# Seven block products for the attention output projection, with all of adaLN's remaining groups moved beside the retention's projections

## The chip, the cores and the metric

The program runs on one core of one Trainium2 chip. The core has five engines: TensorE (PE in the profile, with its weight loads as PEld), VectorE (DVE), ScalarE (ACT), GpSimd (POOL) and SyncE (SP), and 16 DMA engines. The metric is the device time of one launch in microseconds, the median of several runs.

## The reference

One layer of a hybrid backbone, run for 128 context tokens and 512 latent tokens, 640 in all. Everything is float32. What matters here, cut from the reference:

```
m  = silu(cond) @ w_mod + b_mod            # adaLN: sh1, sc1, g1, sh2, sc2, g2 (1024 columns each)
h  = rmsnorm(x, norm1_g) * (1 + sc1) + sh1
q, k, v, rq, rk, rv, rg, ga, gr = split(h @ w_in)
ya = attend_blocks(q, k_all, v_all)        # 640 x 1024
yr = silu(rg) * rms_scale(retention)       # 640 x 1024
y  = sigmoid(ga) * (ya @ w_att_o) + sigmoid(gr) * (yr @ w_ret_o)
x  = x + g1 * (y @ w_out)
x  = x + g2 * conv_ffn(rmsnorm(x, norm2_g) * (1 + sc2) + sh2)
return rmsnorm(x, final_g)
```

The change touches `ya @ w_att_o` (640 x 1024 by 1024 x 1024), the place of the products `silu(cond) @ w_mod` that are not needed at the start, the end of `yr @ w_ret_o`, and the end of the last normalisation.

## The kernel before

Every float32 product is made of three matmuls on a split: a number is written as a high part that TensorE takes as it is (`fp32r`) and a low part, the rest. `mm3` adds high by high, high by low and low by high into one PSUM bank. `w_split` (L139) makes the two parts of a weight: ACT casts the high part (L145), DVE subtracts it for the low part (L150), or, in the form called "dma", ACT writes the negative high part (L147) and a DMA on POOL's queue adds the weight to it.

**Attention projection** (L795 and around). The attention output is split into `yaT` (high `ya.u1`, low `ya.u2`, transposed, 8 chunks of 128 rows by 640 tokens; ACT L646, DVE L647). The loop over the 8 output columns of 128 takes the weights of two columns at a time and calls `b_col`, which for each half of 320 tokens makes 8 chunks x 3 matmuls of 128x320 into one bank (L195 to L197). `ya_ev` (DVE, L793) multiplies the result by the gate and, behind the second half, writes the column to DRAM (POOL, L795). In each column, `next(ada)` steps the generator `mod_rest` (L235 and on): it loads 2 MB of `w_mod` into its one buffer `wm` (SP, L249), yields six times, makes 32 matmuls (64 on record, L257), and turns the result around with a small matmul (L265). Beside the attention projection it makes four such groups, for `sc2` and `sh2`; four more, for `g1` and `g2`, run beside the projections of rk, rq and rv. `decay_consts` (L580 to L601) is a chain of small operations of 128x16 on DVE that makes the constants of the retention. All of this stands in the order that the scheduler finds: it lets PE go from one bank to another where one waits.

**Retention projection** (`ret_unit`, and its pump, inside `tc.manual_schedule`, so that PE, DVE and ACT run in the order in which the code is written). Pairs of columns, p = 0 to 3, are made by seven block products instead of eight, as in Strassen's method (Winograd's form): the 1024 rows of the weights and the two columns make 2 x 2 blocks, the tokens make two halves, and products 1 to 7 of 12 matmuls each work on sums of blocks. The order in a pair is 1, 5, 6, 2, 3, 7, 4, with 4 held back by two places into the next pair. Products 1, 6, 7 and 4 add up in one bank, 2 in another, 5 and 3 in a third; ACT copies the shared bank out behind each product (L1114, L1118, L1122, L1126), and the next one may add only then. `prep` makes the weights of one product (a sum on DVE, L1063; the cast on ACT, L1073; the low part by DVE, L1082, or by DMA, L1080, for product 3 and for product 2 of p > 0). `ret_pump` runs `load` and `prep` ahead by the room in the `wh` buffers. `col` applies the gates, `merge` splits the result for the next product (ACT L1099, DVE L1100). Behind it comes the output projection with `w_out`; the split of the second half of its first weights (`w_split(wo1[0])`, on ACT L145) is left to the scheduler.

**The end.** `last(t, c0, n)` makes the last matmuls of a token block and a range of columns and calls `down_add` (DVE L1427, L1428) and `square` (ACT L1445); `root_sum` and `root` make the 1/rms of token blocks (DVE L1453 to L1466, the power on POOL), and `out` scales and writes 128x512 (ACT L1479 or DVE L1477; SP L1481).

## Time and profile before

| | us |
|---|---|
| median of 3 runs | 1182.92 (1180.72 to 1183.16) |
| the profiled execution | 1182.97 |
| its span, first to last instruction | 1181.1 |
| PE busy | 1148.8 (97%) |
| DVE busy | 772.9 (65%) |
| ACT busy | 589.6 (50%) |
| POOL busy | 184.6 (16%) |

The rows come from one profiled execution. A row of the timeline is one instruction, or some alike that follow each other: its start, its duration, its engine, its line in the code, what it writes and reads, its shape, and in brackets how long its engine had been idle in front of it and what ended that. Matmuls are pipelined: one of 128x320 is shown with 0.31 us, but the next begins 0.15 us later, and this pitch is what counts. A table of stretches gives the busy time of each engine in a window, the clock that TensorE was granted (1.00 is 2.4 GHz, 0.50 is 1.2 GHz), and the share of time in which the DMA engines moved data.

### The profile page before, as it was taken

To read this page: it belongs to the slowest core of one execution; us is meant where nothing else is said; L and a number is where in the kernel's file an instruction comes from. 1 tells how busy PE (TensorE), PEld (TensorE's weight loads), DVE (VectorE), ACT (ScalarE), POOL (GpSimd) and SP (SyncE) were. 2 spreads that over 40 slices of the span, in tenths; PEclk is the share of its full clock that TensorE was granted. 3 is DMA by queue.
4 is the path that set the end of the run, shared out by engine and by line. 5 is a ranking of instruction groups with operands and counts; after the bars stand their busy time and mean duration, and the time that the engine had idled before them with its cause. 6 is when DMAs were issued, how large, how long until landed. Compare 5 with 4: busy or idle time off the path is not lost.

```text
span 1181.1 us, 18387 instructions
## 1 busy us (share of the span) xinstructions
PE 1148.8 (97%) x7269; PEld 1033.2 (87%) x7269; DVE 772.9 (65%) x1431; ACT 589.6 (50%) x1078; POOL 184.6 (16%) x195
## 2 busy tenths in 40 slices
...
GB/s 281 253 146 72 37 36 37 36 39 211 259 189 172 162 98 45 37 37 36 71 38 161 244 123 161 117 107 107 161 134 130 142 137 172 125 114 153 136 114 118
DMA packets 136406, 146.10 MB, mean 124 GB/s; under 512 B 26608, under 2 KB 101952, under 8 KB 136320
## 3 DMA queue, kind: packets, MB, share of 16 engines
...
## 4 chain that ended last, share of the span: by engine, by line
PE 89%; DVE 4%; DMA 2%; ACT 2%; issue 2%; POOL 1%; SPq 0%; DVEq 0%; ACTq 0%; POOLq 0%
DMA weights.wh.181_6253<-weights.raw.168_6022 1%; DMA weights.raw.188_6439<-in_w_out 1%; POOL f0.s.5_3532 L950 0%; DMA weights.wh.157_5915<-weights.raw.151_5778 0%; DMA xin.u1.1_108<-in_x_sample 0%; DVE gt.gt0.5_7310 L1379 0%; DVE acts.u2.2_97 L415 0%; PE mm1.mm.11_300 L159 0%; PE mm7.mm.30_8724 L1547 0%; PE mm7.mm.54_10188 L1547 0%; PE mm7.mm.42_9456 L1547 0%; PE mm7.mm.63_10823 L1547 0%; PE mm7.mm.57_10457 L1547 0%; PE mm7.mm.45_9705 L1547 0%; PE mm7.mm.63_10823 L1550 0%
## 5 line engine op out<-in xcount | busy, mean ns | idle before, releaser
L795 POOL DMA_DIRECT2D spill.u2.2_2893<-f1.s.1_1165 x1 | 0.6, 586 | 130.1 <-DVE mod.u4.4_2852 L586 130.1
L1561 DVE TENSOR_TENSOR t7.u4.4_6979<-t7.u4.4_6979,const.u1.1_70 128x322 f32<-128x322 f32 x10 | 5.0, 496 | 11.8 <-ACT const.u1.1_70 L1560 11.8
L888 DVE SCALAR_TENSOR_TENSOR ret2.u1.1_4329<-ret2.u1.1_4329,const.u13.13_93 64x128 f32<-64x128 f32 x24 | 6.8, 339 | 6.6 <-ACT ret2.u1.1_4329 L881 6.5
L1080 POOL DMA_DIRECT2D weights.wh.157_5915<-weights.raw.151_5778 x1 | 1.3, 1347 | 61.4 <-PE mm3.mm.64_5922 L1112 61.4
L1472 POOL TENSOR_TENSOR x1.u1.1_6477<-x1.u1.1_6477,weights.raw.422_11042 128x512 f32<-128x512 f32 x5 | 8.5, 1702 | 10.3 <-ACT x1.tm.112_11055 L1445 7.5
L890 DVE SCALAR_TENSOR_TENSOR ret2.u1.1_4329<-ret2.u1.1_4329,const.u13.13_93 64x128 f32<-64x128 f32 x24 | 6.6, 384 | 4.8 <-ACT ret2.u1.1_4329 L883 4.8
L841 DVE TENSOR_TENSOR ret.u5.5_3535<-ret.u5.5_3535,ret.u1.1_3528 128x512 f32<-128x512 f32 x5 | 3.5, 692 | 9.4 <-POOL ret.r2k.8_3713 L839 3.3
L841 DVE TENSOR_TENSOR ret.u4.4_3534<-ret.u4.4_3534,ret.u1.1_3528 128x512 f32<-128x512 f32 x5 | 3.5, 693 | 9.0 <-POOL ret.r2k.11_3893 L839 4.7
L565 POOL TENSOR_TENSOR p1.u1.1_609<-p1.u3.3_613,p1q.u1.1_603 128x512 f32<-128x512 f32 x1 | 1.3, 1310 | 45.5 <-DMA p1.vc.6_618<-in_cache_v 45.5
L374 PE MATMUL mm1.mm.1_167<-const.u1.1_70,xin.u1.1_108 128*128 128x128 f32 x4 | 1.1, 434 | 7.0 <-DVE xin.u1.1_108 L365 7.0
L150 DVE TENSOR_TENSOR weights.wh.108_4359<-weights.raw.106_4356,weights.wh.107_4358 128x1024 fp32r<-128x1024 f32 x1 | 1.2, 1225 | 10.3 <-ACT weights.wh.107_4358 L145 10.3
L412 ACT CAST acts.u1.1_96<-f0.s.2_110 128x640 fp32r<-128x640 f32 x4 | 2.9, 728 | 10.1 <-DVE f0.s.2_110 L410 10.1
L412 ACT CAST acts.u1.1_96<-f0.s.1_109 128x640 fp32r<-128x640 f32 x4 | 2.9, 726 | 10.1 <-DVE f0.s.1_109 L410 10.1
L145 ACT CAST weights.wh.112_4514<-weights.raw.111_4512 128x1024 fp32r<-128x1024 f32 x1 | 1.1, 1050 | 13.3 <-PE mm3.mm.36_4227 L158 13.3
...
L260 DVE COPY mod2.wr.9_4319<-aux3.aux.15_4286 128x128 f32<-128x128 f32 x1 | 0.3, 292 | 10.9 <-PE aux3.aux.15_4286 L257 10.9
L950 POOL TENSOR_TENSOR f0.s.5_3532<-f0.s.5_3532,ret2.ny20.11_4911 128x512 f32<-128x512 f32 x5 | 6.0, 1235 | 9.1 <-DVE ret2.ny20.11_4911 L220 9.1
L534 ACT ACTIVATE f0.s.3_715<-f0.s.3_715,p1q.ny20.11_883 128x128 f32<-128x128 f32 x20 | 6.0, 387 | 2.5 <-DVE p1q.ny20.11_883 L218 2.5
L374 PEld LDWEIGHTS mm1.mm.1_167<-const.u1.1_70,xin.u1.1_108 128*128 128x128 f32 x4 | 0.7, 216 | 7.3 <-DVE xin.u1.1_108 L365 7.3
L150 DVE TENSOR_TENSOR weights.wh.195_6649<-weights.raw.189_6441,weights.wh.194_6648 128x1024 fp32r<-128x1024 f32 x1 | 1.2, 1224 | 8.9 <-ACT weights.wh.194_6648 L145 8.9
L1439 DVE TENSOR_TENSOR x1.u1.1_6477<-x1.u1.1_6477,gate.u1.1_6448 128x512 f32<-128x512 f32 x10 | 6.8, 688 | 0.0
L145 ACT CAST weights.wh.67_3366<-weights.raw.66_3364 128x1024 fp32r<-128x1024 f32 x1 | 1.0, 1045 | 11.5 <-PE mm3.mm.8_3145 L196 11.5
...
## 6 DMA issues: line engine op xcount, KB each, us to landing
spill.u1.1_2892<-x1.u1.1_6477 POOLq DMA_DIRECT2D x5, 512.0 KB, 3.7
...
p0.u6.6_131<-in_w_mod SPq DMA_DIRECT2D x2, 1024.0 KB
...
mod.wm.6_2920<-in_w_mod SPq DMA_DIRECT2D x1, 2048.0 KB
mod.wm.8_3073<-in_w_mod SPq DMA_DIRECT2D x1, 2048.0 KB
...
```

The source lines that it names most:

```text
L145: nc.scalar.copy(hi, rv)
L150: (lo_eng or V).tensor_sub(lo, rv, hi.bitcast(F32))
L374: nc.tensor.transpose(xps[t, g][:, j * P:(j + 1) * P], xin[:, t, k * P:(k + 1) * P], ident)
L412: nc.scalar.copy(hT[0][:, k, :], xk)
L534: nc.scalar.activation(x[:, j], x[:, j], AF.Copy, scale=rstd[:, j:j + 1])
L841: V.tensor_mul(z, z, r1[:, t, 0:1, :].to_broadcast([P, 8, 64]))
L888: V.scalar_tensor_tensor(Ss[0:64, hh, st + 1, j], Ss[0:64, hh, st, j], cdsel[0:64, h:h + 1], Ss[0:64, hh, st + 1, j], op0=ALU.mult, op1=AL ...
L890: V.scalar_tensor_tensor(Ss[64:128, hh, 2 - st, j], Ss[64:128, hh, 3 - st, j], cdsel[64:128, h:h + 1], Ss[64:128, hh, 2 - st, j], op0=ALU. ...
L950: nc.gpsimd.tensor_mul(ov, ov, rso[:, 4 * t:4 * t + 4].unsqueeze(2).to_broadcast([P, 4, P]))
L1439: V.tensor_mul(x1[:, t, gs], x1[:, t, gs], gb[:, t == 0, gs])
L1472: eng.tensor_mul(x, x, fg[:, c0:c0 + 512])
L1561: V.tensor_sub(u[1][:, hi_u], u[1][:, hi_u], u3[i])
```

## The change

**1. Attention projection.** Columns 0 and 1 are still made by `b_col`, 96 matmuls. The other six columns are pairs p = 1 to 3 of seven products, 252 matmuls instead of 288, by `seven_unit`, which is the retention's `ret_unit` made general. The sums of the tokens' blocks that products 5, 6, 7 and 3 need are new work (`att_sums`): four sums on DVE (L919, L923, L926, L930), each split by a cast on ACT (`hi_sum`, L912) and a subtraction on DVE (`lo_sum`, L915). The whole part is now inside `tc.manual_schedule`, so its order is that of the code. The first weights of rk are loaded and split in there too.

**2. adaLN.** No group runs beside the attention projection. All eight run beside rk, rq and rv, with two `next(ada)` for each step instead of one.

**3. Retention projection.** It uses the same `seven_unit`; for the first pair (`early`) DVE makes the low part of product 3, which DMA made. The split of `w_out`'s second half is written behind the merges, inside the manual order.

**4. The end.** The matmuls of the last two banks of 256 columns both come first, then the two multiplications, the two additions, each with its square; `root_sum(3, 1)` comes ahead of them, `root(0, 3)` and `out(0, 0)` behind them.

The core of the diff:

```diff
+    def att_sums():
+        s1, s3, s4 = qf[1, 1], qf[1, 0], qf[0, 1]
+        V.tensor_sub(s1, s1, qf[1, 0])
+        hi_sum(1, s1)
+        yield
+        lo_sum(1, s1)
+        V.scalar_tensor_tensor(s1, s1, -1.0, qf[0, 0], op0=ALU.mult, op1=ALU.subtract)
+        hi_sum(2, s1)
+        yield
+        V.tensor_sub(s3, qf[0, 0], s3)
+        hi_sum(3, s3)
+        lo_sum(2, s1)
+        yield
+        V.scalar_tensor_tensor(s4, s1, -1.0, s4, op0=ALU.mult, op1=ALU.subtract)
+        lo_sum(3, s3)
+        yield
...
-    ada = mod_rest((("sc", 1, 4096), ("sh", 1, 3072)), mp, aux)
-    for c in range(KD):
-        if c % 2 == 0:
-            w = load_w(a["w_att_o"][0, :, c * P:(c + 2) * P], 8, 256)
...
-        for _ in b_col(w, cc, yaTk, mm, ya_ev):
-            next(ada, None)
-    run(ada)
+    ar = {1: yq[0, 0], 5: ysum[1], 6: ysum[2], 2: yq[0, 1], 7: ysum[3], 4: yq[1, 1], 3: ysum[4]}
+    units = {p: seven_unit(w_ao[:, 2 * p * P:2 * (p + 1) * P], ar, u_of(p), p == 1, att_fin(p)) for p in range(1, KD // 2)}
+    seq = seven_seq(units)
...
+    with tc.manual_schedule(engines={ET.PE, ET.DVE, ET.Activation}):
+        for c in range(2):
...
+            for n, _ in enumerate(b_col(w, slice(c * P, (c + 1) * P), yaTk, mm, ya_ev)):
+                if n % 2 == 1:
+                    next(sums, None)
+                if c and n == 0:
+                    pump(-1, 4)
+        hi_sum(4, qf[0, 1])
+        lo_sum(4, qf[0, 1])
+        ut.append(f0())
+        seven_run(units, seq, pump)
+        wrk.append(load_w(w_in[512:, O_RK:O_RK + 512], 4, 512))
...
-    ada = mod_rest((("g", 0, 2048), ("g", 1, 5120)), mp, aux)
+    ada = mod_rest((("sc", 1, 4096), ("sh", 1, 3072), ("g", 0, 2048), ("g", 1, 5120)), mp, aux)
...
+            next(ada, None)
             next(ada, None)
...
-            if m == 3 or m == 2 and p:
+            if m in (2, 3) and not early:
                 nc.scalar.activation(lo, src, AF.Copy, scale=-1.0)
                 nc.gpsimd.dma_start(lo, src, accum_op=ALU.add)
             else:
                 lows.append(lambda: V.tensor_sub(lo, src, hi.bitcast(F32)))
...
+        seven_run(units, seq, pump, tl_load)
         wo1 = [w_raw(w_out[512:, :512], 4, 512), w_raw(w_out[:512, 512:], 4, 512)]
+        wo0.append(w_split(wo1[0], 4, 512))
...
         last(4, 0, 512)
+        root_sum(3, 1)
+        for c0 in (512, 768):
+            last_mm(4, c0, 256, (0, 1, 2, 3))
+        tms = [down_mul(bank[4, c0], 4, c0) for c0 in (512, 768)]
+        for c0, tm in zip((512, 768), tms):
+            V.tensor_add(x1[:, 4, c0:c0 + 256], x1[:, 4, c0:c0 + 256], tm)
+            square(4, c0, 256)
         root(0, 3)
-        root_sum(3, 1)
         out(0, 0)
-        last(4, 512, 256)
-        last(4, 768, 256)
         out(1, 0)
```

How the order of the engines changes, at three places.

**The attention projection.** On ACT before, behind the splits of the attention output (L646), only whole weight casts (L145) stand beside three small operations of the decay constants:

```order
L646 CAST ya.u1.1_2828<-f0.s.4_964 128x640 x4
L145 CAST weights.wh.59_3056<-weights.raw.56_3050 128x1024
L582 ACTIVATE mod.u2.2_2850<-mod.u2.2_2850 128x16
L145 CAST weights.wh.62_3209<-weights.raw.61_3207 128x1024
L597 ACTIVATE const.u13.13_93<-const.u12.12_92 128x8
L600 ACTIVATE const.u14.14_94<-const.u14.14_94 128x16
L145 CAST weights.wh.64_3213<-weights.raw.61_3207 128x1024
L145 CAST weights.wh.67_3366<-weights.raw.66_3364 128x1024
L145 CAST weights.wh.69_3370<-weights.raw.66_3364 128x1024
L145 CAST weights.wh.72_3546<-weights.raw.71_3544 128x1024
```

On ACT in the changed kernel, at the last two sums: `wh.57` to `wh.60` are the high parts of the weights of pair 1's products 1, 5, 6 and 2, `ysum.u5` and `ya.u1` receive the high parts of sums 3 and 4, and L826 is the copy of pair 1's product 1 out of its bank `mm.5`; L828 is that of product 5 and L830 that of product 6:

```order
L804 CAST weights.wh.58_2992<-weights.raw.56_2986 128x512
L804 CAST weights.wh.59_2997<-weights.raw.56_2986 128x512
L804 CAST weights.wh.60_2999<-weights.raw.56_2986 128x512
L912 CAST ysum.u5.5_2901<-f0.s.3_715 128x1280
L912 CAST ya.u1.1_2828<-f0.s.4_964 128x4x320
L826 COPY f0.s.5_3050<-mm3.mm.5_3051 128x320
L804 CAST weights.wh.62_3067<-weights.raw.56_2986 128x512
L804 CAST weights.wh.63_3069<-weights.raw.56_2986 128x512
L828 ACTIVATE f0.s.5_3050<-mm3.mm.6_3073 128x320
L804 CAST weights.wh.64_3088<-weights.raw.56_2986 128x512
L804 CAST weights.wh.66_3092<-weights.raw.61_3065 128x512
L830 ACTIVATE f0.s.5_3050<-mm3.mm.5_3051 128x320
```

The copy of product 1 stands behind two casts of sums that are not there before. On DVE in the changed kernel, at the same place, L964 is the gate of a half column of columns 0 and 1, L794 a sum of weights, L813 the low part of a weight, L926 and L930 are sums 3 and 4, and L915 are the low parts of sums 2, 3 and 4:

```order
L794 TENSOR_TENSOR weights.raw.56_2986<-weights.raw.56_2986 128x4x128
L813 TENSOR_TENSOR weights.wh.58_2992<-weights.raw.56_2986,weights.wh.58_2992 128x512
L794 TENSOR_TENSOR weights.raw.56_2986<-weights.raw.56_2986 128x4x128
L813 TENSOR_TENSOR weights.wh.59_2997<-weights.raw.56_2986,weights.wh.59_2997 128x512
L813 TENSOR_TENSOR weights.wh.60_2999<-weights.raw.56_2986,weights.wh.60_2999 128x512
L964 SCALAR_TENSOR_TENSOR f1.s.2_1166<-f1.s.2_1166,mm3.mm.3_2973 128x320
L926 TENSOR_TENSOR f0.s.3_715<-f0.s.3_715 128x4x320
L915 TENSOR_TENSOR ysum.u4.4_2900<-f0.s.4_964,ysum.u3.3_2899 128x1280
L964 SCALAR_TENSOR_TENSOR f1.s.2_1166<-f1.s.2_1166,mm3.mm.4_3019 128x320
L930 SCALAR_TENSOR_TENSOR f0.s.4_964<-f0.s.4_964 128x4x320
L915 TENSOR_TENSOR ysum.u6.6_2902<-f0.s.3_715,ysum.u5.5_2901 128x1280
L915 TENSOR_TENSOR ya.u2.2_2829<-f0.s.4_964,ya.u1.1_2828 128x4x320
```

Before, DVE has the four L793 gates of two columns there, the decay constants and whole weight splits (L150) only. The same small operations of the decay constants stand ahead of this piece in both kernels.

**The end of the retention projection.** On ACT before, `wh.190` and `wh.192` are the split of `w_out`'s second half, L1122 and L1126 the copies of the last pair's products 7 and 4 from the bank `mm.72`, and L1099 the merges:

```order
L145 CAST weights.wh.190_6555<-weights.raw.188_6439 128x1024
L1122 COPY f1.s.15_5330<-mm3.mm.72_6291 128x320
L145 CAST weights.wh.192_6559<-weights.raw.188_6439 128x1024
L1126 COPY f1.s.15_5330<-mm3.mm.72_6291 128x320
L1099 CAST acts.u1.1_96<-f1.s.14_5329 128x128
L1099 CAST acts.u1.1_96<-f1.s.14_5329 128x512
```

On ACT in the changed kernel L834 and L838 are these copies, L1245 the merges and `wh.199` and `wh.201` that split:

```order
L834 COPY f1.s.17_6358<-mm3.mm.69_6345 128x320
L838 COPY f1.s.17_6358<-mm3.mm.69_6345 128x320
L1245 CAST acts.u1.1_96<-f1.s.14_6219 128x128
L1245 CAST acts.u1.1_96<-f1.s.14_6219 128x512
L1245 CAST acts.u1.1_96<-f1.s.13_6218 128x128
L1245 CAST acts.u1.1_96<-f1.s.13_6218 128x512
L1245 CAST acts.u1.1_96<-f1.s.18_6359 128x128
L1245 CAST acts.u1.1_96<-f1.s.18_6359 128x512
L1245 CAST acts.u1.1_96<-f1.s.17_6358 128x128
L1245 CAST acts.u1.1_96<-f1.s.17_6358 128x512
L145 CAST weights.wh.199_6499<-weights.raw.197_6495 128x1024
L145 CAST weights.wh.201_6503<-weights.raw.197_6495 128x1024
```

The split went from in front of the two copies and between them to behind the last merge.

**The end of the kernel.** On ACT before, L1479 are outputs and L1445 squares; the last two squares are the 256-wide ones:

```order
L1445 ACTIVATE x1.tm.128_11161,x1.u3.3_6479<-x1.u1.1_6477 128x512
L1479 ACTIVATE x1.u1.1_6477<-x1.u1.1_6477,t7.ry.30_11128 128x512 x2
L1445 ACTIVATE x1.tm.130_11191,x1.u3.3_6479<-x1.u1.1_6477 128x256
L1479 ACTIVATE x1.u1.1_6477<-x1.u1.1_6477,t7.ry.30_11128 128x512
L1445 ACTIVATE x1.tm.132_11209,x1.u3.3_6479<-x1.u1.1_6477 128x256
L1479 ACTIVATE x1.u1.1_6477<-x1.u1.1_6477,t7.ry.34_11169 128x512 x2
```

On ACT in the changed kernel (L1571 are the outputs, L1537 the squares):

```order
L1537 ACTIVATE x1.tm.126_11198,x1.u3.3_6543<-x1.u1.1_6541 128x512
L1537 ACTIVATE x1.tm.128_11217,x1.u3.3_6543<-x1.u1.1_6541 128x512
L1537 ACTIVATE x1.tm.131_11256,x1.u3.3_6543<-x1.u1.1_6541 128x256
L1537 ACTIVATE x1.tm.132_11259,x1.u3.3_6543<-x1.u1.1_6541 128x256
L1571 ACTIVATE x1.u1.1_6541<-x1.u1.1_6541,t7.ry.30_11184 128x512 x3
L1571 ACTIVATE x1.u1.1_6541<-x1.u1.1_6541,t7.ry.33_11221 128x512 x2
```

All outputs now stand behind the last squares; on SP their transfers stand in this order too.

## Rows read from the trace of the kernel before

**Rows 1.** Table of stretches: window, its length, busy time of each engine, granted clock, DMA.

```profile
263.00:329.00 66.00, 66.00 (x651) 64.21 (x650) 29.20 (x73) 13.55 (x20) 3.85 (x7) 1.00 0.63 227
...
620.00:670.00 50.00, 45.68 (x300) 44.93 (x299) 35.20 (x57) 27.60 (x57) 13.22 (x13) 0.97 0.91 194
...
667.00:671.00 4.00, 3.89 (x17) 3.89 (x18) 1.78 (x3) 1.46 (x4) 0.00 (x0) 0.57 0.63 153
...
1100.00:1182.00 82.00, 70.63 (x387) 62.91 (x385) 66.20 (x116) 41.23 (x77) 17.29 (x14) 0.96 0.47 121
```

**Rows 2.** Timeline of PE over the attention projection; an adaLN group; rk's first matmul.

```profile
263.45 0.31 PE L195 MATMUL mm3.mm.1_2904<-ya.u1.1_2828,weights.wh.52_2896 128*128 128x320 f32 x1
...
263.60 0.31 PE L195 MATMUL mm3.mm.2_2935<-ya.u1.1_2828,weights.wh.52_2896 128*128 128x320 f32 x1
...
276.09 1.95 PE L257 MATMUL aux3.aux.1_3001<-mod.wm.6_2920,mod.s128.5_2917 128*32 128x128 f32 x64
...
329.19 0.47 PE L157 MATMUL mm3.mm.17_3539<-weights.wh.72_3546,acts.u1.1_96 128*128 128x512 f32 x1
```

**Rows 3.** Timeline of DVE: attention output's low parts, decay constants, gate, 128x1280, weight's low part.

```profile
266.15 3.02 DVE L647 TENSOR_TENSOR ya.u2.2_2829<-f0.s.4_964,ya.u1.1_2828 128x640 fp32r<-128x640 f32 x4
...
272.09 0.18 DVE L589 TENSOR_TENSOR mod.u2.2_2850<-mod.u2.2_2850,mod.u4.4_2852 128x16 f32<-128x16 f32 x1
...
272.30 0.18 DVE L590 TENSOR_SCALAR mod.u2.2_2850<-mod.u2.2_2850 128x16 f32<-128x16 f32 x1
...
274.69 0.48 DVE L793 SCALAR_TENSOR_TENSOR f1.s.2_1166<-f1.s.2_1166,mm3.mm.3_2962 128x320 f32<-128x320 f32 x1
...
568.93 1.49 DVE L1017 TENSOR_TENSOR rt.u1.1_5323<-yr.u1.1_5318 128x1280 f32<-128x1280 f32 x1
...
612.50 0.69 DVE L1082 TENSOR_TENSOR weights.wh.154_5841<-weights.raw.151_5778,weights.wh.154_5841 128x512 fp32r<-128x512 f32 x1 [0.69 <-ACT weights.wh.154_5841 L1073]
```

**Rows 4.** Timeline of ACT: a cast of 128x1280 and a copy out of a bank.

```profile
573.56 1.26 ACT L1028 CAST rt.u2.2_5530<-rt.u1.1_5323 128x1280 fp32r<-128x1280 f32 x1 [1.01 <-DVE rt.u1.1_5323 L1019]
...
616.12 0.42 ACT L1114 COPY f1.s.9_5324<-mm3.mm.63_5899 128x320 f32<-128x320 f32 x1 [1.32 <-PE mm3.mm.63_5899 L1112]
```

**Rows 5.** Timelines of PE and ACT at the two stalls of the retention projection.

```profile
621.34 0.30 PE L1111 MATMUL mm3.mm.64_5922<-yr.u2.2_5319,weights.wh.157_5915 128*128 128x320 f32 x1
...
622.59 0.42 PE L1112 MATMUL mm3.mm.64_5922<-yr.u1.1_5318,weights.wh.157_5915 128*128 128x320 f32 x1 [0.95 <-DMA weights.wh.157_5915<-weights.raw.151_5778]
...
663.34 0.40 PE L159 MATMUL mm3.mm.75_6490<-weights.wh.184_6325,acts.u2.2_97 128*128 128x512 f32 x1
...
665.69 1.04 ACT L145 CAST weights.wh.190_6555<-weights.raw.188_6439 128x1024 fp32r<-128x1024 f32 x1 [4.49 <-DMA weights.raw.188_6439<-in_w_out]
...
666.64 0.42 ACT L1122 COPY f1.s.15_5330<-mm3.mm.72_6291 128x320 f32<-128x320 f32 x1
...
667.11 0.47 PE L1109 MATMUL mm3.mm.72_6291<-yr.u1.1_5318,weights.wh.183_6288 128*128 128x320 f32 x1 [3.37 <-ACT f1.s.15_5330 L1122]
...
667.38 0.47 PE L1111 MATMUL mm3.mm.72_6291<-yr.u2.2_5319,weights.wh.183_6288 128*128 128x320 f32 x1
```

**Rows 6.** Table of stretches: an adaLN load of 2 MB in the retention's projections.

```profile
352.00:358.00 6.00, 6.00 (x28) 4.91 (x27) 2.02 (x4) 1.48 (x3) 2.23 (x4) 1.00 0.94 343
```

**Rows 7.** Timelines of PE, ACT, SP and DVE at the end; the stretch of the output transfers.

```profile
1170.35 0.28 PE L159 MATMUL acc7.acc.57_11193<-weights.wh.420_11037,gt.gt1.28_10983 128*128 128x256 f32 x1
...
1170.96 1.33 ACT L1479 ACTIVATE x1.u1.1_6477<-x1.u1.1_6477,t7.ry.30_11128 128x512 f32<-128x512 f32 x2 [0.83 <-DVE t7.rm.32_11167 L1453]
...
1171.04 0.41 DVE L1427 TENSOR_TENSOR x1.tm.129_11188<-acc7.acc.56_11175,gate.u1.1_6448 128x256 f32<-128x256 f32 x1
...
1171.71 0.36 SPq L1481 DMA_DIRECT2D out_y_prompt<-x1.u1.1_6477  x1
...
1176.43 0.75 DVE L1477 SCALAR_TENSOR_TENSOR x1.u1.1_6477<-x1.u1.1_6477,t7.ry.30_11128,weights.raw.422_11042 128x512 f32<-128x512 f32 x1
...
1173.00:1179.00 6.00, 0.00 (x0) 0.00 (x0) 4.03 (x10) 1.93 (x5) 0.54 (x1) 0.74 0.97 368
```

324 lines of the change are left out of this document (189 added, 135 removed).

## The prediction, made before the changed kernel was run

> **What bounds the kernel now.** I read the views from coarse to fine. First the table of stretches: TensorE (PE) is busy all of the 66 us of the attention projection, 45.68 of the 50 us of the retention projection, and 70.63 of the last 82 us, most of which lies behind its last matmul [rows 1]. So PE sets the time nearly everywhere, and what the change can win is matmuls left out, PE's stalls in the retention projection, and the end. What it can lose is the cover under which VectorE (DVE) and ScalarE (ACT) work in the attention projection: DVE 29.20 of 66 us, ACT 13.55 [rows 1].
>
> Then PE's rows there. Two banks start side by side at 263.45 and .60, a third right behind; rk's first matmul is at 329.19; a group of adaLN matmuls takes 1.95 [rows 2]. The pitch of a 128x320 matmul is about 0.147, so 8 columns x 48 = 384 of them take 56.4 us and end, without adaLN, at 319.9; the other 9.3 us are the four adaLN groups. Last, the rows of DVE and ACT give the prices of what is added [rows 3, 4], and those around PE's two stalls in the retention projection and those of the end give the rest [rows 5, 7]. The profiled execution took 1182.97 us with a span of 1181.1, so 1.87 lie outside it; the median of the runs is 1182.92, so I make the sum against 1182.97 without a correction.
>
> **Part 1, matmuls saved.** Three pairs take 7 products x 12 matmuls = 84 instead of 96: 36 x 0.147 = -5.3 us, if PE never waits.
>
> **Part 2, the start of the projection.** Before, PE fills the wait for the split of the attention output with three banks in turn [rows 2]. Now its order is by hand: 24 matmuls of the first bank, then 24 of the second. The low parts come from DVE, four 128x640 ones from 266.15 for 3.02, to 269.17 [rows 3]. The first bank's last matmuls cannot come sooner, so the second begins near 269.5 where unhindered it would at 263.45 + 24 x 0.147 = 267.0: +2.5 us.
>
> **Part 3, the sums that the seven products need, and who waits for them.** This decides the case. Products 1, 6, 7 and 4 of a pair add into one bank, and 6 may start only when ACT has copied product 1 out. On ACT that copy stands behind both casts of the sums (the 128x1280 and the 128x4x320 one); the second needs the sum that DVE makes in its third row from the end of the piece printed above. So product 6 waits for nearly all of DVE's list. From the first bank's result on (DVE free at 269.17, three small operations of 0.21, 269.8) this list is, in the order of the program:
> - six 128x1280 operations at 1.49 [rows 3]: 8.9 (the four sums and the low parts of the first two; the forms of 128x4x320 and with a scalar are taken as dear)
> - four gates 128x320 at 0.48: 1.9
> - 28 small 128x16 or 128x8 ones of the decay constants, one per 0.21: 5.9
> - three weight sums at 0.69 (128x512, taken as dear as the 128x512 low part): 2.1; four low parts at 0.69: 2.8
> Together 21.6, so 291.4. Rows overlap by up to 0.08 each, and one round trip to ACT costs 0.69 [rows 3]; I take 291.0. Then ACT's cast 1.26 and its copy 0.42 [rows 4]: 292.7, and product 6 starts at 292.8. PE is ready for it far earlier: 269.5 + 72 x 0.147 = 280.1 for the two columns, product 1 waits some 0.4 and product 5 some 1.4 for the low parts of their weights, and with 24 x 0.147 they end at 285.4. So PE stands 7.4 us.
>
> From 292.8 there are 348 - 120 = 228 matmuls left: 33.5 us, 326.3. DVE and ACT now hold pair 2's weight splits late: ACT has eight casts and copies behind the late copy, so pair 1's product 4 and pair 2's product 6, in whose banks an ACT copy must come first, lose about 2 us (three casts that no product covers), and pair 2's product 7 some 0.3. I take 2.3 (bounds 0 and 4), and the projection ends at 328.6 instead of 319.9: **+8.7**. Bounds: with DVE rows overlapped throughout and no such loss, 324.8 (+4.9); with two more round trips and 4 us, 331 (+11). A slow clock may come on top: an idle of 3.4 us was followed by twelve matmuls at a pitch of 0.267, with the granted clock 0.57 over 667 to 671 [rows 1, 5], 1.2 instead of 2.4 GHz for most of it; that is 1.4 us, which the later wait for ACT would swallow, so I price it at 0 and leave up to 1.5 in the range.
>
> A rule bears on this. In the retention projection, made of the same products, one bank shared by four products cost one visible wait, of 3.5 us, when a copy stood behind a cast [rows 5]. The Trainium skill, "Perfetto Trace Analysis", section "Matmuls", says that independent groups of matmuls should go through different banks so that emptying one overlaps the next. Here 6 adds onto 1 and is not independent, so the rule speaks against the layout without offering a way out; by it the sum would be that of rival A.
>
> **Part 4, adaLN moved.** Four groups leave the attention projection (-9.3) and join the four in rk, rq and rv (+9.3). Each needs a load of 2 MB into the one buffer, issued when the group before has read it. With two steps for one, the groups lie 48 matmuls of 128x512 apart, 48 x 0.23 = 11.1 us. Such a load kept the queues at 0.94 of their time and 343 GB/s from 352 to 358 [rows 6], 6 to 7 us with its issue: it fits with 4 us to spare, less where a 1 MB weight load shares the queue (an estimate of 3 us, 1.05 MB at the same 343 GB/s). Cost 0; up to +3 if two or three are late by 1 us.
>
> **Part 5, the retention projection.** Two stalls. (a) The matmul at 622.59 came 1.25 behind that at 621.34 and waited for the low part of a weight that DMA adds up; now DVE makes it (0.69 more on DVE, which is busy for 35.20 of 50 us [rows 1, 5]): -1.1. (b) PE stood from 663.6 to 667.11, since ACT, in order, held the copy that frees the bank (666.64) behind the cast of w_out's second half, which began at 665.69 when its load had landed. Twelve matmuls then ran at 0.267 [rows 5]. Now the two casts stand behind all merges, so nothing with a late load is in front of the copy: -(667.11 - 663.57) = -3.5, -12 x (0.267 - 0.147) = -1.4. What is late next is that half of w_out; it is needed only when 60 matmuls with the first half are done (13.8 us), while eight casts (taken as dear as the 128x320 copy, 0.42 [rows 4]) and two of 1.04 stand in front: covered. Sum **-6.0**; the bounds are -7 and, if the merges or the load hold PE again, -3.
>
> **Part 6, the end.** PE ends at 1170.6. Before, ACT begins the first of the outputs at 1170.96 and SP issues its transfer at 1171.71; DVE's last output begins at 1176.43 [rows 7] and the span ends at 1181.1. Now the four operations on the last 256 columns come first on DVE and the roots of tokens 0 to 383 behind them, so the first output begins at 1170.6 + 4 x 0.41 + some 0.5 for the root = 1172.8, 1.8 us later, while the last DVE output begins 0.3 to 0.5 sooner. Ten transfers of 256 KB, 2.62 MB, follow. The queues moved 368 GB/s from 1173 to 1179 [rows 7], so they need 7.1 us, nearly all of the 8 us that the tail of transfers has. So the later start counts more than the sooner finish, though the transfers now follow each other more closely: **+0.9**, bounds -0.5 and +1.8.
>
> **Sum.** 1182.97 + 8.7 + 0 - 6.0 + 0.9 = 1186.6 us. The 8.7 is 2.5 + 7.4 + 1.8 + 2.3 of waits (14.0) less 5.3 of matmuls.
>
> **The rivals.** *A, product 6 is not held.* If the copy ran as soon as product 1 is done, PE would lose only part 2's 2.5: 1182.97 - 5.3 + 2.5 - 6.0 + 0.9 = 1175.1. For it: PE was busy throughout here and saving its work is what a PE-bound stretch rewards [rows 1]; against it: the order of ACT printed above. The Trainium skill, "Perfetto Trace Analysis", section "Identifying the Most-Contended Engine", would have the engine with the highest occupancy improved first; PE has it, and by that rule the answer is this time. *B, held for less, and no loss later.* The lower bounds of part 3 and of the end: 1182.97 + 4.9 - 6.0 + 0.3 = 1182.2, within 0.2% of no change. It decides if DVE's list ends before 289 and pair 2 waits for nothing; for it, the overlap of its rows. *C, adaLN's loads come late as well.* A weight load in front of three or four of them costs 1 us each and the slow clock of part 3 is paid in full: 1186.6 + 4 = 1190.6. It decides where a load takes more than 11.1 us. *D, part 5 gains half*, since another copy or merge holds PE in its place: 1186.6 + 3.0 = 1189.6.
>
> **How the numbers follow.** A measurement tells 0.2%, 2.4 us, from no change: faster is below 1180.6, slower above 1185.3. Chances: forecast 0.45 (of it 0.06 below 1185.3), A 0.18, B 0.22, C 0.11, D 0.04. So faster 0.18; within 0.2% 0.22 + 0.06 = 0.28; slower 0.39 + 0.15 = 0.54. The forecast's own range is 1183.5 to 1189.5. The range for 8 in 10 leaves out A below and about 0.02 above: 1178.0 to 1191.0.
>
> **What would show it.** Part 3: PE idle for about 7 us near 285 to 293 in front of pair 1's product 6, the copy of product 1 (L826) near 292 behind a 128x4x320 cast (L912); if that idle is under 2 us, A holds. Part 2: the second bank's first matmul at 269 to 270. Part 4: no idle in front of the adaLN matmuls. Part 5: no gap over 0.5 us in the retention projection. Part 6: the first output's issue 1 to 2 us further behind PE's end. The prediction is wrong if DVE gets through its list while PE still has work, that is before about 285.

## The result

The changed kernel takes 1187.62 us (median of 7, 1186.9 to 1188.18) against 1183.12 for the kernel before (median of 7), a ratio of 1.0039 with a 95% interval of 1.0029 to 1.0050: slower by 0.4%. The prediction was 1186.6. The profiled execution took 1187.62 with a span of 1185.8, against 1182.97 and 1181.1 before, so the two traces differ by 4.7 us of span.

Where they go can be read from four marks on PE, in the timeline of the changed kernel: the first matmul of the attention projection, the first one of the retention projection, the first transposition's tile behind the output projection (`aux.91`), and PE's last matmul.

```profile
262.97 0.31 PE L195 MATMUL mm3.mm.1_2915<-ya.u1.1_2828,weights.wh.52_2905 128*128 128x320 f32 x1
...
622.08 0.31 PE L821 MATMUL mm3.mm.60_5948<-yr.u1.1_5375,weights.wh.161_5881 128*128 128x320 f32 x1
...
720.66 0.60 PE L1344 MATMUL aux3.aux.91_6853<-const.u1.1_70,gt.gt0.1_6552 128*128 128x128 f32 x4
...
1173.78 0.28 PE L159 MATMUL acc7.acc.57_11238<-weights.wh.429_11093,gt.gt1.28_11039 128*128 128x256 f32 x1
```

The same marks stand at 263.45, 614.15, 718.28 and 1170.35 before. The table is worked out from these and from the spans of 1181.1 and 1185.8. The first line of it is no part of the change: over all runs the projection starts between 262.5 and 263.5.

| stretch | before | changed | difference | forecast |
|---|---|---|---|---|
| start to the attention projection | 263.45 | 262.97 | -0.5 | 0 |
| attention projection, adaLN, retention up to its projection | 350.70 | 359.11 | +8.4 | +8.7 |
| retention projection and output projection | 104.13 | 98.58 | -5.5 | -6.0 |
| MLP, to PE's last matmul | 452.07 | 453.12 | +1.0 | 0 |
| PE's last matmul to the end of the span | 10.75 | 12.02 | +1.3 | +0.9 |

**The attention projection.** PE's timeline there shows the first matmul of the second bank, of pair 1's products 1, 5 and 6, the third of product 5, the second of product 6 on the low part of the sum, and the rk matmul behind the projection.

```profile
269.15 0.31 PE L195 MATMUL mm3.mm.2_2943<-ya.u1.1_2828,weights.wh.52_2905 128*128 128x320 f32 x1
...
279.71 0.31 PE L821 MATMUL mm3.mm.5_3051<-ya.u1.1_2828,weights.wh.57_2988 128*128 128x320 f32 x1
...
281.47 0.31 PE L821 MATMUL mm3.mm.6_3073<-ysum.u1.1_2897,weights.wh.58_2992 128*128 128x320 f32 x1
...
281.96 0.42 PE L824 MATMUL mm3.mm.6_3073<-ysum.u1.1_2897,weights.wh.58_2992 128*128 128x320 f32 x1
...
291.58 0.64 PE L821 MATMUL mm3.mm.5_3051<-ysum.u3.3_2899,weights.wh.59_2997 128*128 128x320 f32 x1 [7.88 <-ACT f0.s.5_3050 L826]
...
292.01 0.47 PE L823 MATMUL mm3.mm.5_3051<-ysum.u4.4_2900,weights.wh.59_2997 128*128 128x320 f32 x1
...
328.01 0.40 PE L157 MATMUL mm3.mm.14_3454<-weights.wh.81_3332,acts.u1.1_96 128*128 128x512 f32 x1
```

The second bank begins at 269.15 (forecast 269.5). Product 1 follows without a gap; product 5 loses 0.3 us from its third matmul on (281.96), which waits for the low part of its weights, ready at 281.91, and its last matmul starts at 283.39. Then PE stands until 291.58, 8.0 us at the pitch of a matmul (7.88 in the row), where the forecast had 7.4, until 292.8: the row names the copy L826 as what it waited for. Against [rows 2] this is where PE's unbroken row of matmuls is gone. The table of stretches gives the clock:

```profile
263.00:325.00 62.00, 53.57 (x334) 50.95 (x334) 51.23 (x96) 30.51 (x55) 8.70 (x10) 0.92 0.40 97
...
286.00:291.00 5.00, 0.00 (x0) 0.00 (x0) 5.00 (x5) 2.52 (x2) 0.55 (x1) 0.50 0.17 66
...
293.00:294.00 1.00, 1.00 (x6) 1.00 (x5) 1.00 (x3) 0.00 (x0) 0.00 (x0) 0.50 0.00 0
...
296.00:300.00 4.00, 4.00 (x28) 4.00 (x28) 3.21 (x6) 1.46 (x3) 0.00 (x0) 0.97 0.83 258
...
620.00:670.00 50.00, 49.79 (x337) 49.10 (x336) 35.45 (x58) 29.39 (x62) 12.30 (x11) 1.00 0.73 148
```

PE is busy 53.57 of 62 us where [rows 1] had 66 of 66; DVE rises to 51.23. The granted clock is 0.50 (1.2 GHz) over 286 to 291, in the idle time, and still over 293 to 294, with the matmuls back; over 296 to 300 it is 0.97, nearly all of it at 1.00. The last row answers to [rows 1] for the retention projection: 49.79 of 50 us instead of 45.68, and no stretch at half clock.

From the start to the last matmul of the projection, 327.3 (328.01 less a triple of rk's matmuls, 0.69, that stands among them), there are 64.4 us where 348 matmuls at 0.1467 (the pitch to one more digit) are 51.1. The 13.3 us are 2.65 at the start (269.15 - 262.97 - 3.53), 8.35 up to product 6 (0.3 in product 5, 8.0 behind it), and 2.3 behind it, nearly all of them for matmuls at the slow pitch. The forecast had 14.0.

What held the copy is seen on DVE and ACT, in the rows that answer to the order printed in front of the prediction:

```profile
288.13 1.48 DVE L930 SCALAR_TENSOR_TENSOR f0.s.4_964<-f0.s.4_964 128x1280 f32<-128x1280 f32 x1
...
289.53 1.48 DVE L915 TENSOR_TENSOR ysum.u6.6_2902<-f0.s.3_715,ysum.u5.5_2901 128x1280 fp32r<-128x1280 f32 x1
...
289.72 1.26 ACT L912 CAST ya.u1.1_2828<-f0.s.4_964 128x1280 fp32r<-128x1280 f32 x1 [2.02 <-DVE f0.s.4_964 L930]
...
291.10 0.43 ACT L826 COPY f0.s.5_3050<-mm3.mm.5_3051 128x320 f32<-128x320 f32 x1
```

ACT's cast of sum 4 (L912) ends at 290.98 and the copy (L826) begins at 291.10, as forecast from the order. But a second thing ends at 291.01: DVE's low part of sum 3, which reads `f0.s.3`. Experiments 1, 5 and 6 are about that.

**The end.** SP's first output transfer, DVE's last output and the stretch of the transfers:

```profile
1176.72 0.36 SPq L1573 DMA_DIRECT2D out_y_prompt<-x1.u1.1_6541  x1
...
1179.47 0.75 DVE L1569 SCALAR_TENSOR_TENSOR x1.u1.1_6541<-x1.u1.1_6541,t7.ry.30_11184,weights.raw.431_11098 128x512 f32<-128x512 f32 x1
...
1178.00:1184.00 6.00, 0.00 (x0) 0.00 (x0) 2.18 (x4) 1.15 (x2) 0.00 (x0) 0.50 1.02 382
```

Measured from PE's last matmul, the first transfer is issued 2.9 us behind it (1.4 in [rows 7]) and DVE's last output begins 5.7 behind it (6.1). So both forecasts of part 6 hold (1.8 us later, 0.3 to 0.5 sooner), and the sum is a loss: the transfers start 1.6 us later and then run at 382 GB/s, against 368.

### The profile page after: what moved, and what is told of

It reads as the page before. It is cut to its first block, busy times and chain, and to the rows that moved or that the text cites. A ratio compares the mean times of both kernels' runs of the same rounds, so it can differ in the third digit from the quotient of the medians.

```text
span 1185.8 us, 18405 instructions
## 1 busy us (share of the span) xinstructions
PE 1147.8 (97%) x7233; PEld 1027.2 (87%) x7233; DVE 797.4 (67%) x1464; ACT 607.3 (51%) x1115; POOL 187.9 (16%) x198
## 4 chain that ended last, share of the span: by engine, by line
PE 52%; DVE 7%; ACT 4%; issue 2%; DMA 2%; POOL 1%; DVEq 0%; ACTq 0%; POOLq 0%
DMA weights.raw.391_10296<-in_w_up 1%; DVE x1.u1.1_6541 L1527 0%; DMA weights.raw.404_10549<-in_w_up 0%; POOL f0.s.6_3447 L1131 0%; DMA weights.raw.423_10897<-in_w_down 0%; DVE x1.u1.1_6541 L1532 0%; DVE x1.u1.1_6541 L1531 0%; DVE gt.gt0.5_7366 L1468 0%; DVE weights.raw.404_10549 L1617 0%; PE mm3.mm.69_6345 L821 0%; PE mm7.mm.42_9512 L1639 0%; PE mm7.mm.30_8780 L1641 0%; PE mm7.mm.21_8297 L1639 0%; PE mm7.mm.33_9029 L1639 0%; PE mm7.mm.45_9761 L1639 0%
## 5 line engine op out<-in xcount | busy, mean ns | idle before, releaser
L1653 DVE TENSOR_TENSOR t7.u4.4_7035<-t7.u4.4_7035,const.u1.1_70 128x322 f32<-128x322 f32 x10 | 5.0, 496 | 10.9 <-ACT const.u1.1_70 L1652 10.9
L145 ACT CAST weights.wh.111_4287<-weights.raw.110_4285 128x1024 fp32r<-128x1024 f32 x1 | 1.0, 1047 | 13.7 <-issue 13.7
L145 ACT CAST weights.wh.121_4571<-weights.raw.120_4569 128x1024 fp32r<-128x1024 f32 x1 | 1.1, 1050 | 13.3 <-PE mm3.mm.33_4284 L158 13.3
L145 ACT CAST weights.wh.101_3993<-weights.raw.100_3991 128x1024 fp32r<-128x1024 f32 x1 | 1.0, 1047 | 13.3 <-PE mm3.mm.23_3700 L158 13.3
L260 DVE COPY mod2.wr.17_4376<-aux3.aux.15_4343 128x128 f32<-128x128 f32 x1 | 0.3, 291 | 10.9 <-PE aux3.aux.15_4343 L257 10.9
```

The lines of the kernel that those rows point to most:

```text
L145: nc.scalar.copy(hi, rv)
L1653: V.tensor_sub(u[1][:, hi_u], u[1][:, hi_u], u3[i])
```

## The experiments

Times are compared as ratios to the kernel before on the same chip; it had medians of 1181.99 (runs 1 to 4), 1183.54 (5 to 8) and 1183.71 (9 to 12); the changed kernel's own ratio is 1.0039.

| run | us | ratio to before (95%) | start of projection to retention projection | to `aux.91` | last matmul to end |
|---|---|---|---|---|---|
| before | | 1 | 350.7 | 104.1 | 10.8 |
| changed | 1187.62 | 1.0039 (1.0029 to 1.0050) | 359.1 | 98.6 | 12.0 |
| 1 cast of sum 4 behind | 1189.19 | 1.0061 (1.0046 to 1.0076) | 360.8 | 99.1 | 11.8 |
| 2 decay constants behind | 1186.86 | 1.0043 (1.0028 to 1.0058) | 357.8 | 99.3 | 11.8 |
| 3 old projection | 1178.65 | 0.9970 (0.9958 to 0.9982) | 350.7 | 98.3 | 12.2 |
| 4 old end | 1186.39 | 1.0040 (1.0026 to 1.0055) | 359.5 | 98.3 | 10.8 |
| 5 own buffer | 1189.00 | 1.0043 (1.0028 to 1.0058) | 359.6 | 98.3 | 11.9 |
| 6 buffer and order | 1187.83 | 1.0037 (1.0024 to 1.0050) | 358.7 | 99.0 | 11.9 |
| 7 sums early | 1184.58 | 1.0009 (0.9999 to 1.0018) | 355.4 | 99.3 | 11.8 |
| 8 adaLN alone | 1184.32 | 1.0001 (0.9991 to 1.0010) | 351.9 | 105.2 | 10.9 |
| 9 split alone | 1178.10 | 0.9960 (0.9948 to 0.9973) | 350.7 | 100.0 | 10.7 |
| 10 old projection, old end | 1178.57 | 0.9963 (0.9949 to 0.9976) | 350.7 | 98.9 | 11.2 |
| 12 four plain columns | 1179.61 | 0.9970 (0.9957 to 0.9982) | 350.4 | 98.3 | 10.9 |

The three last columns are differences of the same marks on PE in each run's trace. Run 12 is called so by its label; there is no run 11. Line numbers in the rows of a run are those of that run's kernel, which shift by a few.

**1. The cast of sum 4 behind the copy.** Theory: product 6 is held by ACT's order.

```diff
-        hi_sum(4, qf[0, 1])
-        lo_sum(4, qf[0, 1])
+        def late_sum(n):
+            if n == 0:
+                hi_sum(4, qf[0, 1])
+                lo_sum(4, qf[0, 1])
-        seven_run(units, seq, pump)
+        seven_run(units, seq, pump, late_sum)
```

> The changed kernel with one move: the cast and the low part of the fourth sum are written behind pair 1's first product, so that on ACT the copy of product 1 stands in front of the cast of sum 4. Theory (product 6 is held by ACT's order, not by the bank or the weights): the copy then waits only for the cast of sum 3, which ended at 287.7 us, so product 6 starts near 288.3 instead of 291.58 and PE's idle time falls from 7.9 to about 4.7 us; product 3, which now needs the late sum 4, starts near 293.5 instead of 297.3; time about 3.5 us under the changed kernel, near 1184. Rival (weights and bank pace hold product 6 anyway): product 6 stays at 291.5, time unchanged, 1187.6.

It did not fall: 1189.19, and product 6 where it was. The timelines of PE and ACT of this run:

```profile
291.52 0.64 PE L821 MATMUL mm3.mm.5_3049<-ysum.u3.3_2899,weights.wh.59_2997 128*128 128x320 f32 x1 [7.88 <-ACT f0.s.5_3048 L826]
...
291.04 0.43 ACT L826 COPY f0.s.5_3048<-mm3.mm.5_3049 128x320 f32<-128x320 f32 x1 [3.40 <-DVE ysum.u6.6_2902 L915]
```

ACT now stands in front of the copy for 3.40 us with nothing else to do, and the row names what it waits for: `ysum.u6`, DVE's L915, the low part of sum 3. The copy writes `f0.s.5`, and that buffer is the one of `f0.s.3`, half of the attention output, which L915 is the last to read. So the copy has two holders, and they end within 0.03 us of each other in the changed kernel. The stretch is 1.6 us longer than in the changed kernel. Of that, 0.6 is the half clock, which lasts until 297.6 here (296.2 there), and most of the rest are small waits at pair 2's products 6 and 7, whose copies come later on ACT. The ratio's interval overlaps that of the changed kernel, so the rise is seen in the trace alone.

**2. The decay constants behind the projection.** This tests the sum of part 3, which counted 28 small operations as 5.9 us of DVE's list.

```diff
-    decay_consts(dec, dtmp)
...
         wrk.append(load_w(w_in[512:, O_RK:O_RK + 512], 4, 512))
+        decay_consts(dec, dtmp)
```

> The changed kernel with the small operations of the decay constants written behind the whole attention projection instead of among the sums. Theory A, as the prediction summed it (DVE's list is work through and through, 28 small operations x 0.21 = 5.9 us of it): product 6 starts 5.9 us earlier, near 285.7, no slow clock behind it, time about 7.5 us lower, near 1180. Theory B (DVE's list is a chain with holes: it waits for the second bank's end at 272.7 and for ACT's casts of sum 2 and of the first weight, 1.9 us, and the small operations fill these holes): product 6 comes only about 1.1 us earlier, near 290.5, idle 6.8 us, time 1 to 1.5 us lower, near 1186.3.

Theory B, by the start of product 6; the ratio, 1.0043 against 1.0039, does not tell the theories' small difference in time. DVE's timeline of the run (sum 1, the gate of the second bank, the low part of the first weight), and PE's row of product 6:

```profile
269.58 1.49 DVE L918 TENSOR_TENSOR f0.s.4_964<-f0.s.4_964,f0.s.3_715 128x1280 f32<-128x1280 f32 x1
...
272.69 0.49 DVE L963 SCALAR_TENSOR_TENSOR f1.s.1_1165<-f1.s.1_1165,mm3.mm.2_2908 128x320 f32<-128x320 f32 x1 [1.63 <-PE mm3.mm.2_2908 L197]
...
277.96 0.69 DVE L813 TENSOR_TENSOR weights.wh.57_2953<-weights.raw.56_2951,weights.wh.57_2953 128x512 fp32r<-128x512 f32 x1 [1.85 <-ACT weights.wh.57_2953 L804]
...
290.43 0.63 PE L821 MATMUL mm3.mm.5_3016<-ysum.u3.3_2864,weights.wh.59_2962 128*128 128x320 f32 x1 [7.22 <-ACT f0.s.5_3015 L826]
```

Without the small operations DVE waits 1.63 us for the second bank and 1.85 us for ACT, in the places in which they stood, and product 6 comes at 290.43, 1.15 us earlier; the stretch is 1.3 us shorter. The list is a chain with holes, and most of the 5.9 us lay in the holes.

**3. The old projection.** The attention projection and adaLN as before, the rest as changed.

```diff
-    ada = mod_rest((("sc", 1, 4096), ("sh", 1, 3072), ("g", 0, 2048), ("g", 1, 5120)), mp, aux)
+    ada = mod_rest((("g", 0, 2048), ("g", 1, 5120)), mp, aux)
...
+    for c in range(KD):
...
+        for _ in b_col(w, cc, yaTk, mm, ya_ev):
+            next(ada, None)
+    run(ada)
```

> The changed kernel with its first two parts undone: the attention projection in eight whole columns, four adaLN groups beside it and four beside rk, rq and rv, as before; the retention projection and the end stay as changed. Theory (the projection alone loses, 7.4 us up to its end and 0.5 us more until the retention projection; the rest gains 4): time near 1187.6 - 7.9 = 1179.7, 3.4 us under the kernel before. Rival (the loss lies in what comes later, and the retention's gain is not there without the new order): time within 2 us of the kernel before or above it.

1178.65, 0.3% under the kernel before, which is the theory's 3.4 us. The stretch up to the retention projection is back at 350.7, and the retention part's gain stays (98.3). So the first two parts of the change cost 8.4 us, and the gain behind them does not depend on them.

**4. The old end.**

```diff
-        root_sum(3, 1)
-        for c0 in (512, 768):
-            last_mm(4, c0, 256, (0, 1, 2, 3))
...
+        root(0, 3)
+        root_sum(3, 1)
+        out(0, 0)
+        last(4, 512, 256)
+        last(4, 768, 256)
```

> The changed kernel with the end in the old order (the first root and output in front of the last two banks of 256 columns). Theory (the later start of the transfers costs): PE's end to the end of the span falls by about 1.3 us back to 10.2 us, time near 1186.3. Rival (the sooner finish of DVE is worth as much): unchanged, 1187.6, or up to 0.5 us higher.

The last column is back at 10.8, 1.2 us less. It is 10.7 to 10.9 in the other runs with the old end (8, 9 and 12; run 10 has 11.2), and 11.8 to 12.2 in every run with the new one. The time itself is 1.2 us under the changed kernel's 1187.62, but those were on different chips and the ratios (1.0040, 1.0039) don't tell them apart. So the marks in the trace carry this verdict, not the time.

**5 and 6. A buffer of its own, alone and with the cast behind.** With run 1 and the changed kernel these make the four corners of two holders.

```diff
+    own = ysp([P, TOK])
...
-                return ut[0][:, 2 * (p % 2) + f]
+                return own if p == 1 and f == 0 else ut[0][:, 2 * (p % 2) + f]
```

> The changed kernel with one move: pair 1's first column gets a buffer of its own (128x640), so that the copy of product 1 need not wait for the last reader of the attention output (the low part of sum 3 on DVE, which ended at 291.01 us), whose buffer it otherwise overwrites. Theory (the copy has two holders that end together: that reader at 291.01 and ACT's cast of sum 4 in front of it at 290.98): with one left, product 6 still starts near 291.5, time unchanged, 1187.6. Rival (the buffer was the only holder): product 6 starts near 288.3 and the time falls by 3 us.

> Both moves together: the buffer of its own, and the cast of sum 4 behind the copy. Theory of two holders: now the copy waits only for ACT's cast of sum 3 (end 287.7), product 6 starts near 288.3, idle 4.7 us; product 3 waits for the late low part of sum 4 until about 293.5; time 3 to 3.5 us under the changed kernel, near 1184.3. Rival (a third holder, the weights): product 6 at 291.5 again, 1187.6 or above, as with the order alone (1189.2).

Alone it changed nothing: product 6 at 291.14 (the projection began 0.26 us earlier there), with the copy right behind the cast of sum 4. PE's and ACT's rows of run 5:

```profile
291.14 0.64 PE L821 MATMUL mm3.mm.5_3052<-ysum.u3.3_2899,weights.wh.59_2998 128*128 128x320 f32 x1 [7.66 <-ACT ysum.u7.7_2913 L826]
...
289.51 1.26 ACT L912 CAST ya.u1.1_2828<-f0.s.4_964 128x1280 fp32r<-128x1280 f32 x1 [2.02 <-DVE f0.s.4_964 L930]
...
290.67 0.42 ACT L826 COPY ysum.u7.7_2913<-mm3.mm.5_3052 128x320 f32<-128x320 f32 x1
```

Together they let product 6 start at 288.2, as the theory said. But the time stayed, ratio 1.0037. PE's rows of run 6:

```profile
288.22 0.63 PE L821 MATMUL mm3.mm.5_3050<-ysum.u3.3_2899,weights.wh.59_2998 128*128 128x320 f32 x1 [4.38 <-ACT ysum.u7.7_2913 L826]
...
302.87 0.41 PE L821 MATMUL mm3.mm.5_3050<-ya.u1.1_2828,weights.wh.64_3089 128*128 128x320 f32 x1 [1.32 <-ACT ysum.u7.7_2913 L834]
...
305.31 0.42 PE L821 MATMUL mm3.mm.8_3177<-ysum.u3.3_2899,weights.wh.68_3116 128*128 128x320 f32 x1 [0.41 <-ACT f0.s.5_3049 L826]
```

The idle time in front of product 6 falls to 4.38 us (from 7.88), and the matmuls behind it still run at half clock (0.267 apart). Then PE waits 1.32 and 0.41 us at pair 1's product 4 and pair 2's product 6, where the changed kernel had no wait, since the copies there (L834, L826) stand behind weight splits that had to wait for DVE. With two smaller waits, at the product 7 of either pair, that comes to 3.0 us at the pitch of a matmul, of the 3.5 by which product 6 had been earlier, counted from the start of the projection. Two of these copies on ACT, L834 of pair 1 and L830 of pair 2, in the changed kernel (first two rows) and in run 6:

```profile
302.30 0.42 ACT L834 COPY f0.s.5_3050<-mm3.mm.5_3051 128x320 f32<-128x320 f32 x1
...
310.46 0.43 ACT L830 ACTIVATE f0.s.5_3050<-mm3.mm.8_3176 128x320 f32<-128x320 f32 x1
...
302.40 0.41 ACT L834 COPY ysum.u7.7_2913<-mm3.mm.5_3050 128x320 f32<-128x320 f32 x1
...
310.56 0.43 ACT L830 ACTIVATE f0.s.5_3049<-mm3.mm.8_3177 128x320 f32<-128x320 f32 x1
```

They come at the same time in both (the projection starts 0.13 us later in run 6), although product 6 starts 3.4 us earlier. So the chain of DVE and ACT runs on at its own pace. In run 6 pair 2's product 7 starts right behind its copy, at 311.04; in the changed kernel it starts 0.5 us behind it, at 311.39, so little more than that was to be won. Both theories of that expectation are right in half: two holders, and no third one at product 6, but DVE and ACT are behind by then, and the wait moves to the next place.

**7. The sums early.**

```diff
         V.tensor_sub(s1, s1, qf[1, 0])
         hi_sum(1, s1)
+        V.tensor_sub(s3, qf[0, 0], s3)
+        hi_sum(3, s3)
         yield
         lo_sum(1, s1)
         V.scalar_tensor_tensor(s1, s1, -1.0, qf[0, 0], op0=ALU.mult, op1=ALU.subtract)
         hi_sum(2, s1)
-        yield
-        V.tensor_sub(s3, qf[0, 0], s3)
-        hi_sum(3, s3)
+        lo_sum(3, s3)
         lo_sum(2, s1)
         yield
         V.scalar_tensor_tensor(s4, s1, -1.0, s4, op0=ALU.mult, op1=ALU.subtract)
-        lo_sum(3, s3)
```

The moves of runs 1 and 2 are in it as well.

> The changed kernel with the sums in another order (sum 3 right behind sum 1 while ACT casts sum 1, all low parts of sums 1 to 3 in front of the weights, the cast of sum 4 behind product 1's copy) and the decay constants behind the projection. Theory (the loss is the order of DVE's and ACT's chains and not their amount of work): product 1's copy waits for nothing but its turn behind four weight casts, product 6 starts near 283.8 with under 1 us of idle, the clock stays at 1.00, product 3 waits about 1.8 us for sum 4, the projection ends 8 us earlier, near 319; time near 1179.5. Rival (DVE has too much to do: 18 us of it between 269.5 and product 6's turn, and the wait only moves): a wait of 4 us or more at products 3, 7 or pair 2, time 1183 or above.

The rival's time, 1184.58, with the theory's start: product 6 comes at 283.59. PE's rows behind it are products 3 and 7 of pair 1 and its product 4:

```profile
283.59 0.41 PE L821 MATMUL mm3.mm.5_3014<-ysum.u3.3_2864,weights.wh.59_2966 128*128 128x320 f32 x1 [0.48 <-ACT f0.s.5_3013 L826]
...
288.54 0.41 PE L821 MATMUL mm3.mm.6_3038<-ya.u1.1_2828,weights.wh.62_3032 128*128 128x320 f32 x1 [1.17 <-ACT f0.s.5_3013 L828]
...
292.01 0.42 PE L821 MATMUL mm3.mm.5_3014<-ysum.u5.5_2866,weights.wh.63_3034 128*128 128x320 f32 x1 [0.98 <-ACT f0.s.5_3013 L830]
...
298.99 0.41 PE L821 MATMUL mm3.mm.5_3014<-ya.u1.1_2828,weights.wh.64_3053 128*128 128x320 f32 x1 [1.44 <-ACT f0.s.5_3013 L834]
```

There is no long gap any more and the clock is at 1.00 in every window from 283 to 320, so the 2.3 us of slow matmuls are gone. But product after product waits 0.5 to 1.4 us for an ACT copy, each of which stands behind casts that follow a DVE operation. The stretch is 355.4: 3.7 us won of 8.4. The copy L830 of pair 2 ends 44.6 us from the start of the projection here and 47.9 in the changed kernel, and runs 1 and 2 fit too (49.7 and 46.9, with stretches of 360.8 and 357.8): the stretch follows the end of this chain, within half a microsecond. This order brings it forward by 3.3 us. What is left, some 7 us of waits in front of PE, is a chain of work and of passes from one engine to the other, with DVE busy 26.45 of the 31 us from 269 to 300 and ACT 14.67; whether a better order would shorten it further was not tested.

**8. adaLN alone.** The kernel before with all eight groups beside rk, rq and rv.

```diff
-    ada = mod_rest((("sc", 1, 4096), ("sh", 1, 3072)), mp, aux)
...
-        for _ in b_col(w, cc, yaTk, mm, ya_ev):
-            next(ada, None)
-    run(ada)
+        run(b_col(w, cc, yaTk, mm, ya_ev))
...
-    ada = mod_rest((("g", 0, 2048), ("g", 1, 5120)), mp, aux)
+    ada = mod_rest((("sc", 1, 4096), ("sh", 1, 3072), ("g", 0, 2048), ("g", 1, 5120)), mp, aux)
...
+            next(ada, None)
             next(ada, None)
```

> The kernel before with the second part of the change alone: all eight adaLN groups beside rk, rq and rv, two steps at a time, none beside the attention projection, which stays at eight whole columns. Theory (moving costs nothing or up to 0.5 us, as in the changed kernel, where one turn-round of a group waited 0.5 us): within 1 us of the kernel before, about 1182.4. Rival (loads of 2 MB into one buffer come late): 2 to 5 us over the kernel before.

Ratio 1.0001. The stretch grows by 1.2 us; PE's timeline has one wait for a load in it (and one of 0.5 us, as in the changed kernel, for a group's turn-round):

```profile
399.08 1.95 PE L257 MATMUL aux3.aux.11_4016<-mod2.wm.12_3953,mod2.s128.1_3401 128*32 128x128 f32 x64 [0.51 <-DMA mod2.wm.12_3953<-in_w_mod]
```

Of eight loads one is late, by 0.5 us. Part 4 priced them at 0 with up to 3 on top. In the changed kernel no load was late. The 105.2 of the next column is not adaLN's: the stall in front of the bank's copy in the retention projection, 3.37 us in [rows 5], is 4.44 in this trace.

**9. The split alone.** The kernel before with one line of the change.

```diff
         wo1 = [w_raw(w_out[512:, :512], 4, 512), w_raw(w_out[:512, 512:], 4, 512)]
+        wo0.append(w_split(wo1[0], 4, 512))
...
-                first=(lambda: [x + y for x, y in zip(*wo0[1:])], lambda: w_split(wo1[0], 4, 512))))
+                first=(lambda: [x + y for x, y in zip(*wo0[1:3])], lambda: wo0[3])))
```

> The kernel before with one line of the change: the split of w_out's second half is written behind the merges of the retention projection, in the manual order. Theory (that cast in front of the bank's copy made the stall at 663.6 and the slow clock behind it): the gap of 3.5 us in front of 667.11 and the twelve matmuls at 0.267 go, the gap of 1.1 us at 622.6 stays; time 4.5 to 5 us under the kernel before. Rival (the half is then late where it is needed, or the merges hold PE instead): 0 to 2 us under it.

1178.10, 0.4% under the kernel before, 5.6 us by the medians and 4.7 by the ratio, as the theory had it. ACT's timeline shows the bank's copy, which stood behind the cast in [rows 5]; PE's shows the first stall, which is left, and a new wait; the table of stretches shows the clock.

```profile
662.92 0.42 ACT L1122 COPY f1.s.15_5330<-mm3.mm.72_6291 128x320 f32<-128x320 f32 x1 [1.79 <-PE mm3.mm.72_6291 L1112]
...
622.45 0.41 PE L1112 MATMUL mm3.mm.64_5922<-yr.u1.1_5318,weights.wh.157_5915 128*128 128x320 f32 x1 [0.93 <-DMA weights.wh.157_5915<-weights.raw.151_5778]
...
675.59 1.16 PE L275 MATMUL aux3.aux.90_6475<-const.u1.1_70,const.u5.5_85 128*128 128x128 f32 x8 [0.96 <-ACT gate.u1.1_6456 L277]
...
660.00:664.00 4.00, 4.00 (x27) 3.70 (x26) 3.27 (x7) 1.25 (x3) 0.89 (x2) 1.00 0.92 268
...
664.00:668.00 4.00, 4.00 (x35) 4.00 (x34) 1.66 (x3) 1.14 (x3) 0.07 (x1) 1.00 0.96 296
```

The copy runs at 662.92 as soon as product 7 is done, PE is busy all of 660 to 668, and the clock stays at 1.00. The stall at 622.45 stays. The retention projection alone, first to last matmul, takes 51.1 us instead of 55.9, 4.8 less; 0.7 of that comes back in the output projection, where PE now waits 0.96 us for ACT at 675.59, a wait that the kernel before does not have.

**10. Old projection and old end.** The edits of runs 3 and 4 together: of the change the retention part and the moved split are left.

> The changed kernel with projection and adaLN as before and the end as before, so that only the retention projection is changed (the split behind the merges, and product 3's low part of the first pair on DVE). Theory: 5.5 us under the kernel before, by the two stalls and the slow clock, and 1.2 us under the kernel with the old projection and the new end (which stood 3.3 us under the kernel before). Rival (the two undone parts interact): not below that kernel.

0.9963, 4.4 us under the kernel before where 5.5 was expected, and level with run 9 (0.9960): the low part of the first pair's product 3, made by DVE here and by a DMA in run 9, cannot be told in the time, though the retention part is 1.1 us shorter in the trace (98.9 against 100.0; half of that is the first stall gone, half a shorter wait at `aux.90`). Against run 3 the time fell by 0.07% of the kernel before and not by 0.1%, within the intervals.

**12. Four plain columns.**

```diff
-        for c in range(2):
+        for c in range(1, 4):
...
-    units = {p: seven_unit(..., p == 1, att_fin(p)) for p in range(1, KD // 2)}
+    units = {p: seven_unit(..., p == 2, att_fin(p)) for p in range(2, KD // 2)}
```

Column 0 is written out with its two halves side by side, and the moves of run 7 and the old end are in it.

> A version built from what the runs showed: four whole columns first and only two pairs by seven products (360 matmuls instead of 348), the first column's two halves side by side, the sums early, decay constants behind the projection, the cast of sum 4 behind the first copy, the old end; adaLN beside rk, rq and rv as changed. Theory (DVE's and ACT's chain for sums and first weights, some 20 us, needs PE work of that length in front of it; four columns give 28 us): no wait over 1 us in the projection, which ends near 316 instead of 319.9 before and 327.3 in the changed kernel; time 8 to 9 us under the kernel before. Rival (DVE and ACT cannot feed seven products at any time here, also in the last pairs): waits of 4 us or more remain and the time is not below the kernel with the old projection and the old end.

1179.61, 3.5 us under the kernel before by the ratio, less than half of what was expected. The first pair's products 1, 5, 6, 2, 3 and 7 now follow each other without a wait, where run 7 with the same order of the sums and less work of PE in front had three: that work was what they lacked. The first column, with its halves side by side, loses 0.5 us to the split of the attention output instead of 2.65. Two waits are left, of PE on ACT's copies:

```profile
307.19 0.41 PE L821 MATMUL mm3.mm.9_3130<-ya.u1.1_2828,weights.wh.69_3169 128*128 128x320 f32 x1 [1.30 <-ACT f0.s.5_3129 L834]
...
309.64 0.42 PE L821 MATMUL mm3.mm.12_3255<-ysum.u3.3_2864,weights.wh.73_3196 128*128 128x320 f32 x1 [0.42 <-ACT f0.s.5_3129 L826]
```

So the theory failed by the last pair, and the rival's second half holds: the time is not below run 10 (0.9970 against 0.9963), which has eight plain columns. The projection ends at 318.6, 1.3 us before the kernel before's 319.9 and not 4, and 0.8 of that counted from its start. With 0.5 us for adaLN the stretch is 350.4, level with eight plain columns. In this run's trace the MLP is 2.5 us longer than before, with two idle times of 0.91 and 0.70 us, one for a weight's low part that a DMA adds up, one for ACT; why they come here is open.

## Why the prediction held, step by step

*Part 1* (-5.3): 36 matmuls fewer, at the pitch as read.

*Part 2* (+2.5): 2.65.

*Part 3*, the wait: forecast 7.4 with product 6 at 292.8; measured 8.0 with 291.58. The place, the copy and its position on ACT were right. Two things in the working were not. It named one holder where there are two: the buffer of the attention output, which the copy overwrites, is read by DVE until 291.01, and taking away either holder alone gains nothing (runs 1 and 5). The order of instructions showed the one and not the other; that the pair's columns get their buffer from the two-buffer pool that holds the attention output stood in the code. And it added up DVE's operations as if they left no holes. The sum came near, 291.0 forecast for DVE against 289.6, because in this kernel the small operations fill the places where DVE would otherwise wait; as a price of these operations, 5.9 us, it is wrong (run 2: 1.15).

Of the two small waits at products 1 and 5 (1.8) only 0.3 came, at product 5: the low parts were ready at 279.3 and 281.9. This and the longer idle time together are 8.35, against 9.2 forecast.

*The 2.3 us behind the wait*: the same size by luck. The forecast had them as waits at pair 1's product 4 and pair 2's products 6 and 7, and the slow clock for nothing, since a wait would swallow it. In the changed kernel the loss is the slow clock, and no such wait follows. The two do exchange, as the forecast said, but the other way round: the copies on ACT come when DVE's and ACT's chain lets them (run 6), so had the matmuls run at full clock, product 4 would have been there at 302.1, in front of the end of its copy at 302.7, and pair 2's products 6 and 7 likewise. By these rows some 1.7 of the 2.3 us would have come back as waits; this is an estimate, and no run shows the same order at full clock. What bounds the projection's end is thus less the wait in front of product 6, which the forecast made its main term, than the chain of weight splits behind it: run 6 took 3.5 us out of that wait and gained 0.4.

*Part 4* (0): 0.5 in the changed kernel, for a turn-round that the forecast did not name, and 1.2 alone, of which one late load is the larger half. Right within its bounds.

*Part 5* (-6.0): -5.5. Run 9 shows that the line that moves the split is worth most of it: 4.8 us in the retention projection, as summed (3.5 + 1.4), and 4.1 of the stretch's 104.1 us after the new wait on ACT, which the forecast did not have. The low part made by DVE is worth 0.6 of the 1.1 (run 10 against run 9, in the retention projection).

*Part 6* (+0.9): 1.3, by the mechanism described. The 1.0 us in the MLP had no step; that stretch is 0.1 to 2.5 us longer than in the kernel before over the runs, whose matmuls there are the same, and what sets it is open.

*The rivals.* A, product 6 not held, would have been 1175.1; it is excluded. The Trainium skill, "Perfetto Trace Analysis", section "Identifying the Most-Contended Engine", would improve the engine with the highest occupancy first, and it judges TensorE's headroom by, among others, the busy share of its weight loads. By that rule fewer matmuls on a PE that is 97% busy, with weight loads for 64.21 of 66 us [rows 1], gain. The trace disagrees here: the PE work in that stretch hid work of DVE and ACT, and the change took matmuls away, moved adaLN's 9.3 us out of it, and added 22 us to DVE (51.23 against 29.20). B did not come about: DVE's list ended at 289.6, not before 289, and PE stood for 8.0 us. Run 7 comes out at B's time, within 0.2% of no change, but by another order of the sums and with waits spread over several products. C's late loads and D did not come about; C's slow clock did, in place of the waits.
